# Down weights in 8 KB runs with strided transposes; inverse roots as one GpSimd power, small tables queued late, bias split moved to the router's end

## The chip, the cores and the metric

One core of a Trainium2 chip runs the whole layer. The metric is device time in microseconds (us), the median of the runs; every weight is read from HBM once, in float32. TensorE is called PE below (PEld is its weight load), VectorE DVE, ScalarE ACT, GpSimd POOL, and SP the engine whose queue issues nearly all DMAs.

## What is computed

A decoder layer on 256 tokens of width 1024: root-mean-square norm, one projection to seven groups of 512 columns, eight attention heads and four heads of a gated linear recurrence, an output projection, then a mixture of 32 experts (top 4 per token) and a per-layer embedding gate. Cut to what matters here:

```
def rms_norm(x, g):
    y = xf * lax.rsqrt(jnp.mean(xf * xf, axis=-1, keepdims=True) + RMS_EPS)
...
    a = rms_norm(h, mix_norm_g[i]);  z = a @ w_in[i]
    q = partial_rope(rms_norm(q, q_norm_g[i]), positions) * (ATTN_HEAD_DIM ** -0.5)
    k = partial_rope(rms_norm(k, k_norm_g[i]), positions)
...
    o = rms_norm(o, norm_g) * jax.nn.silu(gate)
...
    for e in range(N_EXPERTS):
        gu = t @ w_gu[e] + b_gu[e]
        ...
        y = ((up + 1.0) * glu) @ w_down[e] + b_down[e]
        out = out + gates[:, e:e + 1] * y
```

## The kernel before

The program has a front (norms, projection `zchunk`, attention, recurrence, output projection `wo`, router) and then a loop over the 32 experts, with a short end that applies the embedding gate.

**Weights.** All weights go through one list, `seq`, in the order of their use, as pieces of 1 MB. `fill` issues the next pieces on SP's queue as long as a slot is free; a slot is a piece of SBUF of 8 KB per partition, 19 of them at first (shared with the front's own tensors, which come from the same pool) and two more from the router on. `need` hands a piece to its user, and `used` frees its slot and calls `fill`. A gate/up piece is 128 rows, one row of 2048 numbers per partition, so one run of 8 KB in HBM. A down piece is 256 rows of 1024 numbers, and partition p gets rows p and 128 + p: two runs of 4 KB. In the front each piece of `w_in` and `w_out` is split into a rounded high part (ACT, line 193) and a rest (line 194, on DVE or, for the pieces in `POOL_FIRST`, on POOL).

**The inverse root.** `rsqrt` computes 1/sqrt by a bit trick and three Newton steps: 11 instructions on DVE on tiles of 128x2 to 128x16 (lines 245 to 250). It is used five times: for the rows of x (`row_rstd`), for k and q (`qk_norm`), for the recurrence's output (`hgrn_out`, r8) and for the second norm, whose result (rstd2) the router reads. The k and q norms stand between a projection chunk and the release of its PSUM tile: `pz` has two buffers, and line 608 (N) is the last reader of the chunk.

**Experts.** For each expert, `onehot` and `gather_rows` collect up to 64 tokens on PE, `gather_columns` transposes them, `gate_up` multiplies (line 1009 the bias, line 1016 the weights), `hidden` transposes the product u in four blocks of 128 columns (line 1034), `down` multiplies with the down weights (line 1047), and `scatter` adds to the result (line 1058). The bias is kept as a rounded part and its rest, `bgu`; the rest is made at the router's end on POOL (line 910).

A scheduler orders the instructions of each engine when the program is built. The lists in the section on the change print that order.

Of the kernel before, what the change touches and what calls it, by code (L numbers as in the profile page):

```python
# [11 lines left out]
F32 = mybir.dt.float32  # L12
F32R = mybir.dt.float32r
BF = mybir.dt.bfloat16
I32 = mybir.dt.int32
U32 = mybir.dt.uint32
AF = mybir.ActivationFunctionType
OP = mybir.AluOpType
# [4 lines left out]
E = 32  # L23
# [87 lines left out]
def layer(ctx, tc, A, at):  # L111
# [11 lines left out]
    seq, src = [], {}  # L123
# [10 lines left out]
        for n in range(2):  # L134
            add(("wo", n), hf, w_out, 512 * n)
    w_gu = A["expert_w_gate_up"][0].rearrange("e (j p) n -> e j p n", p=128)
    w_dn = A["expert_w_down"][0].rearrange("e (j k p) n -> e j p k n", p=128, k=2)

    def expert(kind, e):
        w, n = (w_gu, 8) if kind == "GU" else (w_dn, 4)  # L140
# [19 lines left out]
    def fill():  # L160
        while st["raw"] < st["cap"] and st["next"] < len(seq) and S.left() > st["keep"]:
            k = seq[st["next"]]
            st["next"] += 1
            st["raw"] += 1
            if k[0][0] == "GU":
                shape = [128, 2048]
            elif k[0][0] == "D" or k[0] == "pj":
                shape = [128, 2, 1024]
            else:
                shape = [128, 4, 512]  # L170
            t, at_ = S.new(shape, F32, "raw", True)
            sp.dma_start(t, src[k])
            raw[k] = t, at_

    def cap(n, keep=0):
# [58 lines left out]
    sp.dma_start(rows[16:24], A["hgrn_lb_logits"].rearrange("l (j p) -> (l j) p", p=128))  # L234
    gcol = pers.tile([128, 24], F32, name="gcol")

    def lnexp():
        act.preload_act_table_set("natural_log_exp_and_others")

    def rsqrt(y, v, tag):  # L240

        n = v.shape[1]
        a = pers.tile([128, n], F32, name="rs_a" + tag)
        b = pers.tile([128, n], F32, name="rs_b" + tag)
        dve.tensor_scalar(a.bitcast(I32), v.bitcast(I32), 1, None, op0=OP.arith_shift_right)
        dve.tensor_scalar(b.bitcast(I32), a.bitcast(I32), -1.0, float(0x5F3759DF), op0=OP.mult, op1=OP.add)
        for k in range(3):
            dve.scalar_tensor_tensor(a, v, -0.5, b, op0=OP.mult, op1=OP.mult)
            dve.tensor_tensor(a, a, b, OP.mult)
            dve.scalar_tensor_tensor(y if k == 2 else b, a, 1.5, b, op0=OP.add, op1=OP.mult)  # L250

    def row_rstd(tag):
        ss = pers.tile([128, 2], F32, name="ss" + tag)
        junk = S.new([128, 2, D], F32, "junk")
        for tt in range(2):
            act.activation(junk[:, tt, :], h[:, tt, :], AF.Square, accum_out=ss[:, tt:tt + 1])
        S.free()
        vv = pers.tile([128, 2], F32, name="vv" + tag)
        dve.tensor_scalar(vv, ss, 1.0 / D, EPS, op0=OP.mult, op1=OP.add)
        r = pers.tile([128, 2], F32, name="rstd" + tag)  # L260
        rsqrt(r, vv, tag)
        return r

    mx = ExitStack()
# [38 lines left out]
    sp.dma_start(pos_i, A["positions"].rearrange("o (t p) -> p (o t)", p=128))  # L303

    rw = mp.tile([128, 8, E], F32, name="rw")
    pool.dma_start(rw, A["router_w"][0].rearrange("(j p) e -> p j e", p=128))
    rb = mp.tile([128, E], F32, name="rb")
    pool.dma_start(rb, A["router_b"][0:1, :].to_broadcast([128, E]))
    tri = const("tri", q=pool, p=mp)
    slot = const("slot", q=pool)  # L310
    sel2 = const("sel", q=pool)

    p0 = bank()
    pe.transpose(p0[:, :24], rows, ident[:24, :24])
# [231 lines left out]
    def hgrn_out():  # L546
        vh = B["vh"]
        bs = [bank(), bank()]
        for hh in range(4):
            c = slice(hh * 128, hh * 128 + 128)  # L550
            c1 = slice(512 + hh * 128, 512 + hh * 128 + 128)
            pe.matmul(bs[0][:, c], B["A"][:, 0, hh, :], vh[:, c], start=True, stop=True)
            pe.matmul(bs[1][:, c], B["A01"][:, hh, :], vh[:, c], start=True, stop=False)
            pe.matmul(bs[1][:, c], B["A"][:, 1, hh, :], vh[:, c1], start=False, stop=True)
        S.free()
        values_read()
        B["ob"] = bs
        yield
        sq = carve(128)
        s8 = mp.tile([128, 8], F32, name="os8")  # L560
        for tt in range(2):
            for hh in range(4):
                act.activation(sq, bs[tt][:, hh * 128:hh * 128 + 128], AF.Square, accum_out=s8[:, tt * 4 + hh:tt * 4 + hh + 1])
        v8 = mp.tile([128, 8], F32, name="ov8")
        r8 = mp.tile([128, 8], F32, name="or8")
        dve.tensor_scalar(v8, s8, 1.0 / 128, EPS, op0=OP.mult, op1=OP.add)
        rsqrt(r8, v8, "o")
        B["r8"] = r8
        yield

# [24 lines left out]
    def qk_norm(p, gi, dst, scale):  # L595
        N2 = S.new([128, 2, 1024], F32, "N2")
        sq, n = N2[:, 0], N2[:, 1]
        act.activation(sq, p, AF.Square)
        yield
        s16 = mp.tile([128, 16], F32, name="s16")  # L600
        dve.tensor_reduce(s16, sq.rearrange("p (a d) -> p a d", d=64), X, OP.add)
        v16 = mp.tile([128, 16], F32, name="v16")
        dve.tensor_scalar(v16, s16, 1.0 / 64, EPS, op0=OP.mult, op1=OP.add)
        r16 = mp.tile([128, 16], F32, name="r16")
        rsqrt(r16, v16, "q%d" % gi)
        yield
        n3 = n.rearrange("p (a d) -> p a d", d=64)
        dve.tensor_tensor(n3, p.rearrange("p (a d) -> p a d", d=64), r16[:, :, None].to_broadcast([128, 16, 64]), OP.mult)  # L608
        dve.tensor_tensor(n3, n3, qg[:, gi:gi + 1, :].to_broadcast([128, 16, 64]), OP.mult)
        yield  # L610
        if "rt" not in B:
            B["rt"] = carve(384).rearrange("p (a b c d) -> p a b c d", a=2, b=3, c=8)
        r = B["rt"]
        for tt in range(2):
            v = n[:, tt * 512:tt * 512 + 512].rearrange("p (h d) -> p h d", d=64)
            x1, x2 = v[:, :, 0:8], v[:, :, 8:16]
            c = cs[:, tt, 0:1, :].to_broadcast([128, 8, 8])
            s = cs[:, tt, 1:2, :].to_broadcast([128, 8, 8])
            a, b_, c_ = (r[:, tt, k] for k in range(3))
            dve.tensor_tensor(a, x1, s, OP.mult)  # L620
            dve.tensor_tensor(b_, x1, c, OP.mult)
            dve.tensor_tensor(c_, x2, s, OP.mult)
            dve.tensor_tensor(x1, b_, c_, OP.subtract)
            dve.tensor_tensor(b_, x2, c, OP.mult)
            dve.tensor_tensor(x2, b_, a, OP.add)
        yield
        for h2 in range(2):
            b = bank()
            for k in range(2):
                for tt in range(2):  # L630
                    o = tt * 512 + (2 * h2 + k) * 128
                    pe.transpose(b[:, k * 256 + tt * 128:k * 256 + tt * 128 + 128], n[:, o:o + 128], ident)
            act.activation(dst[:, 2 * h2 * 256:2 * h2 * 256 + 512], b, AF.Copy, scale=scale)
        S.free()
        yield
# [181 lines left out]
    logits(1)  # L817
    dve.tensor_tensor(vv2, ss4[:, 0, :], ss4[:, 1, :], OP.add)
    dve.tensor_scalar(vv2, vv2, 1.0 / D, EPS, op0=OP.mult, op1=OP.add)
    rsqrt(rstd2, vv2, "m")  # L820

    S.free(3)
    cap(99)
# [83 lines left out]

    act.activation(bgu, braw, AF.Copy)
    for r in (slice(64, 96), slice(96, 128)):
        pool.tensor_tensor(bgu[r, :], braw[r, :], bgu[r, :].bitcast(F32), OP.subtract)  # L910
    spill()
    S.free(3)
    mx.close()
# [91 lines left out]
    def gate_up(e, between):  # L1005
        G, U = mm(), mm()
        x = R[e]["x"]
        for k, P in enumerate((G, U)):
            pe.matmul(P, R[e]["sel"], bgu[:, k * 512:k * 512 + 512], start=True, stop=False,  # L1009
                      skip_group_check=True)  # L1010
        for j in range(8):
            w, _ = need(("GU", e), j)
            for k, P in enumerate((G, U)):
                for n in range(2):
                    c = k * D + n * 512
                    pe.matmul(P[halves[n], :], x[:, j % 4, j // 4, :], w[:, c:c + 512], start=False, stop=j == 7, skip_group_check=True)  # L1016
            used(("GU", e), j, 0)
            for f in between.get(j, ()):
                f()
        gm = wp.tile([128, 512], F32, name="gm")  # L1020
        sg = wp.tile([128, 512], F32, name="sgm")
        um = wp.tile([128, 512], F32, name="um")
        dve.tensor_scalar(gm, G, 7.0, None, op0=OP.min)  # L1023
        act.activation(sg, gm, AF.Sigmoid, scale=1.702)  # L1024
        dve.tensor_scalar(um, U, 7.0, -7.0, op0=OP.min, op1=OP.max)
        dve.scalar_tensor_tensor(um, um, 1.0, gm, op0=OP.add, op1=OP.mult)
        dve.tensor_tensor(um, um, sg, OP.mult)
        R[e]["u"] = um

    def hidden(e):  # L1030
        u = R[e]["u"]
        b = misc()
        for c in range(4):
            pe.transpose(b[:, c * 128:c * 128 + 128], u[:, c * 128:c * 128 + 128], ident)  # L1034
        t = wp.tile([128, 4, 2, 64], F32, name="ht", bufs=2)
        act.activation(t.rearrange("p c n s -> p (c n s)"), b, AF.Copy)
        R[e]["h"] = t
# [155 lines left out]
```

## Time and profile before

| what | value |
|---|---|
| median of three runs | 1169.43 us (1166.47 to 1170.24) |
| the profiled execution's own time | 1167.22 us |
| its span, first to last instruction | 1165.4 us |
| PE busy | 93% of the span |
| DVE, ACT, POOL busy | 25%, 17%, 6% |
| HBM read | 430.51 MB, 370 GB/s over the span |
| TensorE clock granted, mean | 0.987 of full speed |

The profile is one execution. Busy shares are means over stages with different limits: the front lasts until about 190 us, the experts from there to about 1117 us. The end of a matmul is modelled, so a PE that is busy all the time may still have room.

### The profile page before, as it was taken

The numbers are of one execution on the slowest core, as the hardware profiler recorded it, in microseconds if no ns is written. First come the engines' busy times: TensorE is split into PE (matmuls) and PEld (weight loads), VectorE is DVE, ScalarE is ACT, GpSimd is POOL, SyncE is SP. The second block draws the span as 40 slices with busy tenths as digits, with TensorE's granted clock in tenths as the row PEclk, the third lists the DMA queues.
The fourth block names the chain that finished last, engine by engine and source line by source line (L and its number), as shares of the span: only waits on it lengthen the run. The fifth ranks groups of instructions, "written<-read, shape, count | busy, mean of one in ns | idle before, by whom it ended". The sixth has DMA issues, their size and how long they took to land. (4 is left out here: it accounts for less than half of the span.)

```text
span 1165.4 us, 12337 instructions
## 1 busy us (share of the span) xinstructions
PE 1080.2 (93%) x5001; PEld 451.9 (39%) x5001; DVE 294.1 (25%) x613; ACT 201.9 (17%) x366; POOL 74.8 (6%) x77
## 2 busy tenths in 40 slices
PE   5889988999999999999999999989999999999887
PEld 4778764333333333333333332223333332223226
DVE  4877744211111111111111111101111111110025
ACT  5646531000011011000000000001000000000013
POOL 4433321000000000000000000000000000000000
PEclk9989997999999999999999999999999999999999
DMA  9913568999999999999999999999998999999991
GB/s 313 338 60 103 207 227 324 415 416 417 417 416 417 417 418 418 417 417 418 417 417 417 417 417 417 405 417 417 416 415 327 418 417 417 417 418 417 418 400 46
DMA packets 87118, 432.43 MB, mean 371 GB/s; under 512 B 7736, under 2 KB 9184, under 8 KB 54288
## 3 DMA queue, kind: packets, MB, share of 16 engines
q1 hardware_dynamic: 86480, 430.35, 91.6%
q0 software_dynamic: 576, 1.23, 0.4%
q8 instruction: 41, 0.67, 0.2%
q14 instruction: 21, 0.17, 0.0%
HBM read 430.51 MB, written 1.05 MB: 370 GB/s over the span
## 5 line engine op out<-in xcount | busy, mean ns | idle before, releaser
L1016 PE MATMUL bk<-raw,x 128*64 128x512 f32 x2048 | 473.5, 596 | 12.5 <-DMA raw<-in_expert_w_gate_up 12.3
L1016 PEld LDWEIGHTS bk<-raw,x 128*64 128x64 f32 x2048 | 143.0, 137 | 311.6 <-issue 261.9
L1047 PE MATMUL bk<-raw,ht 128*64 128x512 f32 x1024 | 247.2, 598 | 12.5 <-DMA raw<-in_expert_w_down 12.5
L1047 PEld LDWEIGHTS bk<-raw,ht 128*64 128x64 f32 x1024 | 71.4, 136 | 150.9 <-issue 115.0
L1023 DVE TENSOR_SCALAR gm<-bk 128x512 f32<-128x512 f32 x32 | 22.1, 692 | 364.7 <-PE bk L1016 364.7
L1024 ACT ACTIVATE sgm<-gm 128x512 f32<-128x512 f32 x32 | 20.2, 630 | 422.5 <-DVE gm L1023 422.5
L846 PE MATMUL bk<-h,sx 128*64 128x512 f32 x256 | 66.1, 614 | 9.5 <-ACT st L1002 9.5
L997 DVE TENSOR_SCALAR sg<-c_slot,posx,gates 128x128 f32<-128x128 f32 x64 | 19.3, 344 | 213.1 <-PE bk L1000 213.1
L1058 PE MATMUL pz<-y,st 64*128 64x512 f32 x256 | 66.0, 627 | 4.0 <-ACT y L1051 2.2
L838 POOL CAST sb<-c_sel 128x128 fp32r<-128x128 f32 x32 | 9.3, 293 | 847.9 <-PE bk L1009 832.0
L194 POOL TENSOR_TENSOR lo<-raw,hi 128x1024 fp32r<-128x1024 f32 x20 | 50.1, 2526 | 84.7 <-ACT hi L193 84.7
L859 DVE TENSOR_TENSOR x<-bk,gcol 128x256 f32<-128x256 f32 x64 | 24.2, 420 | 108.8 <-PE bk L855 108.8
L1051 ACT ACTIVATE y<-bk 128x512 f32<-128x512 f32 x32 | 19.1, 597 | 145.5 <-PE bk L1047 145.5
L193 ACT ACTIVATE hi<-raw 128x1024 fp32r<-128x1024 f32 x36 | 37.8, 1056 | 22.9 <-issue 9.7
L1058 PEld LDWEIGHTS pz<-y,st 64*128 64x128 f32 x256 | 22.6, 188 | 45.7 <-issue 40.9
L380 PE MATMUL pz<-hi,ahi 128*128 128x512 f32 x80 | 33.6, 420 | 7.0 <-DVE N L608 6.8
L835 DVE TENSOR_SCALAR sx<-c_slot,posx,rstd 128x64 f32<-128x64 f32 x64 | 17.2, 312 | 79.0 <-PE bk L846 78.9
L848 ACT ACTIVATE xr<-bk 128x512 f32<-128x512 f32 x32 | 19.1, 597 | 93.7 <-PE bk L846 93.7
L382 PE MATMUL pz<-hi,alo 128*128 128x512 f32 x80 | 33.2, 415 | 0.0
L381 PE MATMUL pz<-lo,ahi 128*128 128x512 f32 x80 | 33.0, 412 | 0.0
L846 PEld LDWEIGHTS bk<-h,sx 128*64 128x64 f32 x256 | 17.4, 139 | 38.6 <-issue 24.4
L1002 ACT ACTIVATE st<-bk 128x256 f32<-128x256 f32 x32 | 12.3, 384 | 113.5 <-PE bk L1000 113.5
(266 smaller groups left out, 849.6 us busy)
## 6 DMA issues: line engine op xcount, KB each, us to landing
raw<-in_expert_w_gate_up SPq DMA_DIRECT2D x256, 1024.0 KB, 19.9
raw<-in_expert_w_down SPq DMA_DIRECT2D x128, 1024.0 KB, 20.0
raw<-in_w_in SPq DMA_DIRECT2D x14, 1024.0 KB, 13.6
raw<-in_w_out SPq DMA_DIRECT2D x4, 1024.0 KB, 5.1
raw<-in_ple_gate SPq DMA_DIRECT2D x4, 1024.0 KB, 18.9
h<-in_x SPq DMA_DIRECT2D x2, 512.0 KB, 4.2
ct<-in_consts SPq DMA_DIRECT2D x2, 512.0 KB
raw<-in_ple_proj SPq DMA_DIRECT2D x1, 1024.0 KB, 20.2
```

The lines of the kernel that those rows point to most:

```text
L193: act.activation(hi, w[:, o:o + 2], AF.Copy)
L194: (pool if i in POOL_FIRST else dve).tensor_tensor(lo, w[:, o:o + 2], hi.bitcast(F32), OP.subtract)
L380: pe.matmul(o, ahi[:, j, s], hi[:, jj, :], start=j == 0, stop=False)
L381: pe.matmul(o, ahi[:, j, s], lo[:, jj, :], start=False, stop=False)
L382: pe.matmul(o, alo[:, j, s], hi[:, jj, :], start=False, stop=j == 7)
L846: pe.matmul(b[halves[n], :], s[:, tt, :], h[:, tt, n * 512:n * 512 + 512], start=tt == 0, stop=tt == 1, skip_group_check=True)
L859: dve.tensor_tensor(x[:, :, n, :], b.rearrange("p (c n s) -> p c n s", c=4, n=2)[:, :, n, :], g, OP.mult)
L1016: pe.matmul(P[halves[n], :], x[:, j % 4, j // 4, :], w[:, c:c + 512], start=False, stop=j == 7, skip_group_check=True)
L1023: dve.tensor_scalar(gm, G, 7.0, None, op0=OP.min)
L1024: act.activation(sg, gm, AF.Sigmoid, scale=1.702)
L1047: pe.matmul(P[halves[n], :], t[:, f % 4, f // 4, :], w[:, k, n * 512:n * 512 + 512], start=f == 0, stop=f == 7, skip_group_check=True)
L1058: pe.matmul(acc[tt][n], t[halves[n], tt * 128:tt * 128 + 128], y[halves[n], :], start=e == 0, stop=False, skip_group_check=True)
```

## The change

It does six things. (1) The down weights are read with partition p holding rows 2p and 2p + 1 of the piece, one run of 8 KB; `hidden` therefore transposes every second column of u. (2) `rsqrt` becomes one instruction on POOL, v to the power -0.5. (3) In `row_rstd` the second half of the squares goes from ACT to DVE. (4) The first piece of `w_in` is loaded by two DMAs of half the size. (5) The five small tables (router weights, router bias, tri, slot, sel) go from POOL's DMA queue to SP's, behind the first six pieces. (6) The rest of the bias is made on DVE instead of POOL, and the bias of expert 0 is multiplied after its weights instead of before.

```
-    w_dn = A["expert_w_down"][0].rearrange("e (j k p) n -> e j p k n", p=128, k=2)
+    w_dn = A["expert_w_down"][0].rearrange("e (j p k) n -> e j p k n", p=128, k=2)
...
-            sp.dma_start(t, src[k])
+            if place[k]:
+                sp.dma_start(t, src[k])
+            else:
+                for o in (0, 2):
+                    sp.dma_start(t[:, o:o + 2], src[k][:, o:o + 2])
...
+    power = pers.tile([128, 16], F32, name="power")
+    pool.memset(power, -0.5)
...
-    def rsqrt(y, v, tag):
-
-        n = v.shape[1]
-        a = pers.tile([128, n], F32, name="rs_a" + tag)
-        b = pers.tile([128, n], F32, name="rs_b" + tag)
-        dve.tensor_scalar(a.bitcast(I32), v.bitcast(I32), 1, None, op0=OP.arith_shift_right)
-        dve.tensor_scalar(b.bitcast(I32), a.bitcast(I32), -1.0, float(0x5F3759DF), op0=OP.mult, op1=OP.add)
-        for k in range(3):
-            dve.scalar_tensor_tensor(a, v, -0.5, b, op0=OP.mult, op1=OP.mult)
-            dve.tensor_tensor(a, a, b, OP.mult)
-            dve.scalar_tensor_tensor(y if k == 2 else b, a, 1.5, b, op0=OP.add, op1=OP.mult)
+    def rsqrt(y, v):
+        pool.tensor_tensor(y, v, power[:, :v.shape[1]], OP.pow)
...
-        for tt in range(2):
-            act.activation(junk[:, tt, :], h[:, tt, :], AF.Square, accum_out=ss[:, tt:tt + 1])
+        act.activation(junk[:, 0, :], h[:, 0, :], AF.Square, accum_out=ss[:, 0:1])
+        dve.scalar_tensor_tensor(junk[:, 1, :], h[:, 1, :], 1.0, h[:, 1, :], op0=OP.mult, op1=OP.mult, accum_out=ss[:, 1:2])
...
-    pool.dma_start(rw, A["router_w"][0].rearrange("(j p) e -> p j e", p=128))
+    sp.dma_start(rw, A["router_w"][0].rearrange("(j p) e -> p j e", p=128))
...
-        pool.tensor_tensor(bgu[r, :], braw[r, :], bgu[r, :].bitcast(F32), OP.subtract)
+        dve.tensor_tensor(bgu[r, :], braw[r, :], bgu[r, :].bitcast(F32), OP.subtract)
...
+        def bias():
+            for k, P in enumerate((G, U)):
+                pe.matmul(P, R[e]["sel"], bgu[:, k * 512:k * 512 + 512], start=e > 0, stop=e == 0, skip_group_check=True)
...
-            pe.transpose(b[:, c * 128:c * 128 + 128], u[:, c * 128:c * 128 + 128], ident)
+            o = c // 2 * 256 + c % 2
+            pe.transpose(b[:, c * 128:c * 128 + 128], u[:, o:o + 255:2], ident)
```

On POOL, from the start of the program to the end of the router, the order before was this (`lo` is a split of line 194, `rw` the router's weights, `braw` the raw bias, `sb` an expert's selector).

```order
L306 DMA rw<-in_router_w 128x8x32
L308 DMA rb<-in_router_b 128x32
L225 DMA c_tri<-in_consts 128x128
L741 TENSOR_TENSOR rw<-rw,gcol 128x256
L194 TENSOR_TENSOR lo<-raw,hi 128x1024 x9
L463 MEMSET Adg 128x1024
L194 TENSOR_TENSOR lo<-raw,hi 128x1024 x9
L780 DMA braw<-in_expert_b_gate_up 32x512 x8
L194 TENSOR_TENSOR lo<-raw,hi 128x1024 x2
L838 CAST sb<-c_sel 128x128 x2
L910 TENSOR_TENSOR bgu<-braw,bgu 32x1024 x2
```

The same stretch of POOL's order now has the five powers (line 248: for x, k, q, the recurrence's output and the router).

```order
L248 TENSOR_TENSOR rstdx<-vvx,power 128x2
L198 TENSOR_TENSOR lo<-raw,hi 128x1024 x6
L739 TENSOR_TENSOR rw<-rw,gcol 128x256
L248 TENSOR_TENSOR r_341<-v_339,power 128x16
L198 TENSOR_TENSOR lo<-raw,hi 128x1024 x3
L461 MEMSET Adg 128x1024
L198 TENSOR_TENSOR lo<-raw,hi 128x1024
L248 TENSOR_TENSOR r_576<-v_574,power 128x16
L198 TENSOR_TENSOR lo<-raw,hi 128x1024 x8
L778 DMA braw<-in_expert_b_gate_up 32x512 x8
L248 TENSOR_TENSOR or_1190<-ov_1189,power 128x8
L198 TENSOR_TENSOR lo<-raw,hi 128x1024 x2
```

The tables' DMAs are gone from POOL, each power stands between splits, and the bias's rest is no longer there.

On DVE, at the start of the program, the order now is this (`ssx` are the sums of squares, `vvx` the mean square, `lbm` and `lbe` belong to the recurrence's lower bound and read `gcol`, `mt` is the diagonal that PE's first transposes read).

```order
L254 SCALAR_TENSOR_TENSOR junk,ssx<-h 128x1024
L419 TENSOR_TENSOR lbm<-gcol 128x4
L257 TENSOR_SCALAR vvx<-ssx 128x2
L421 TENSOR_TENSOR lbe<-gcol,lbm 128x4
L422 TENSOR_TENSOR lbe<-gcol,lbm 128x4
L318 TENSOR_SCALAR mt<-c_ident,rstdx 128x128 x2
```

The mean square, which was DVE's first instruction, now stands behind one that waits for `gcol`.

On DVE, at the router's end, the order before was this (`hT` is h transposed, `vv` the mean square, `rs_am` and `rs_bm` the Newton steps).

```order
L801 COPY hT<-bk 128x512
L818 TENSOR_TENSOR vv_1445<-ss_1354 128x2
L819 TENSOR_SCALAR vv_1445<-vv_1445 128x2
L245 TENSOR_SCALAR rs_am<-vv_1445 128x2
L246 TENSOR_SCALAR rs_bm<-rs_am 128x2
L801 COPY hT<-bk 128x512
L248 SCALAR_TENSOR_TENSOR rs_am<-vv_1445,rs_bm 128x2
```

The same place now:

```order
L799 COPY hT<-bk 128x512
L908 TENSOR_TENSOR bgu<-braw,bgu 32x1024 x2
L816 TENSOR_TENSOR vv_1400<-ss_1309 128x2
L799 COPY hT<-bk 128x512
L817 TENSOR_SCALAR vv_1400<-vv_1400 128x2
```

The two bias instructions now stand ahead of the second copy of `hT`, and the Newton steps are gone.

## Rows read from the trace of the kernel before

**Rows 1.** The page: span, GB/s in 40 slices of the span.
```profile
span 1165.4 us, 12337 instructions
...
GB/s 313 338 60 103 207 227 324 415 416 417 417 416 417 417 418 418 417 417 418 417 417 417 417 417 417 405 417 417 416 415 327 418 417 417 417 418 417 418 400 46
```

**Rows 2.** Window 365-700: start:end, length, PE, PEld, DVE, ACT, POOL, clock, DMA share, GB/s.
```profile
365.00:700.00 335.00, 321.25 (x1480) 108.45 (x1476) 55.98 (x120) 33.66 (x60) 3.52 (x12) 1.00 1.02 417
```

**Rows 3.** Waits of PE over the whole span: total us, times, longest.
```profile
PE bk L1047 <- DMA raw<-in_expert_w_down: 12.5, 19, 1.6
PE bk L1016 <- DMA raw<-in_expert_w_gate_up: 12.3, 24, 0.6
```

**Rows 4.** PE's timeline (start, us): the same place of two experts that follow each other.
```profile
398.68 0.63 PE L1034 MATMUL bk<-c_ident,um 128*128 128x128 f32 x4 [0.69 <-DVE um L1027]
...
426.81 0.63 PE L1034 MATMUL bk<-c_ident,um 128*128 128x128 f32 x4 [0.69 <-DVE um L1027]
```

**Rows 5.** Windows, first with only 4 KB runs in flight, then with only 8 KB runs.
```profile
250.00:258.00 8.00, 8.00 (x40) 2.73 (x38) 1.29 (x4) 0.60 (x1) 0.00 (x0) 1.00 1.03 410
...
260.20:278.00 17.80, 17.80 (x84) 6.13 (x82) 1.55 (x4) 1.57 (x3) 0.29 (x1) 1.00 1.01 421
```

**Rows 6.** DMA issues of the down weights; the weight loads of line 1034.
```profile
raw<-in_expert_w_down SPq DMA_DIRECT2D x128, 1024.0 KB, 20.0
...
L1034 PEld LDWEIGHTS bk<-c_ident,um 128*128 128x128 f32 x128 | 13.4, 141 | 36.7 <-issue 18.7 <-PE bk L1047 18.0
```

**Rows 7.** Timeline of the start, DVE and POOL.
```profile
7.08 0.17 DVE L259 TENSOR_SCALAR vvx<-ssx 128x2 f32<-128x2 f32 x1 [7.08 <-ACT junk L256]
...
8.59 0.16 DVE L421 TENSOR_TENSOR lbm<-gcol 128x4 f32<-128x4 f32 x1 [0.93 <-ACT gcol L315]
8.64 0.61 POOL L741 TENSOR_TENSOR rw<-rw,gcol 128x256 f32<-128x256 f32 x1 [3.94 <-ACT gcol L315]
...
10.96 0.48 DVE L320 TENSOR_SCALAR mt<-c_ident,rstdx 128x128 f32<-128x128 f32 x2
```

**Rows 8.** PE's waits in the front (0 to 210 us), columns as in rows 3.
```profile
PE pz L380 <- DVE N L608: 6.8, 2, 3.6
PE bk L806 <- DVE hT L801: 3.1, 2, 2.0
PE bk L584 <- DVE G L578: 2.1, 2, 1.9
```

**Rows 9.** Windows in the front, columns as in rows 2.
```profile
72.80:79.70 6.90, 6.79 (x19) 5.41 (x20) 6.87 (x18) 0.56 (x2) 0.00 (x0) 0.62 0.15 55
...
159.60:164.40 4.80, 4.80 (x14) 3.80 (x15) 1.22 (x2) 0.42 (x1) 0.00 (x0) 0.64 0.80 297
```

**Rows 10.** Timeline of DVE in the k norm.
```profile
37.32 2.46 DVE L603 TENSOR_SCALAR v<-s 128x16 f32<-128x16 f32 x1
...
41.48 2.37 DVE L248 SCALAR_TENSOR_TENSOR rs_aq<-v,rs_bq 128x16 f32<-128x16 f32 x1
...
44.38 1.23 DVE L608 TENSOR_TENSOR N<-pz,r 128x1024 f32<-128x1024 f32 x1
```

**Rows 11.** Timeline of DVE: q norm, the recurrence's output.
```profile
64.57 2.40 DVE L603 TENSOR_SCALAR v<-s 128x16 f32<-128x16 f32 x1
...
71.54 1.23 DVE L608 TENSOR_TENSOR N<-pz,r 128x1024 f32<-128x1024 f32 x1
...
150.08 0.17 DVE L566 TENSOR_SCALAR ov<-os 128x8 f32<-128x8 f32 x1 [1.51 <-ACT mt L563]
...
156.84 2.16 DVE L578 SCALAR_TENSOR_TENSOR G<-bk,or,G 128x128 f32<-128x128 f32 x8
```

**Rows 12.** Timeline of the router's end, DVE and POOL.
```profile
173.85 4.78 POOL L910 TENSOR_TENSOR bgu<-braw,bgu 32x1024 fp32r<-32x1024 f32 x2 [0.61 <-POOL sb L838]
...
176.47 2.19 DVE L245 TENSOR_SCALAR rs_am<-vv 128x2 int32<-128x2 int32 x1
178.77 0.68 DVE L801 COPY hT<-bk 128x512 f32<-128x512 f32 x1
```

More of the change, by code (lines that the diff above doesn't have):

```diff
@@ L260, in row_rstd @@
         r = pers.tile([128, 2], F32, name="rstd" + tag)
-        rsqrt(r, vv, tag)
+        rsqrt(r, vv)
         return r
@@ L305, in layer @@
     rw = mp.tile([128, 8, E], F32, name="rw")
-    pool.dma_start(rw, A["router_w"][0].rearrange("(j p) e -> p j e", p=128))
+    sp.dma_start(rw, A["router_w"][0].rearrange("(j p) e -> p j e", p=128))
     rb = mp.tile([128, E], F32, name="rb")
[L308 to L311, printed above, removed]
+    sp.dma_start(rb, A["router_b"][0:1, :].to_broadcast([128, E]))
+    tri = const("tri", p=mp)
+    slot = const("slot")
+    sel2 = const("sel")
     p0 = bank()
@@ L566, in hgrn_out @@
         dve.tensor_scalar(v8, s8, 1.0 / 128, EPS, op0=OP.mult, op1=OP.add)
-        rsqrt(r8, v8, "o")
+        rsqrt(r8, v8)
         B["r8"] = r8
@@ L604, in qk_norm @@
         r16 = mp.tile([128, 16], F32, name="r16")
-        rsqrt(r16, v16, "q%d" % gi)
+        rsqrt(r16, v16)
         yield
@@ L819, in layer @@
     dve.tensor_scalar(vv2, vv2, 1.0 / D, EPS, op0=OP.mult, op1=OP.add)
-    rsqrt(rstd2, vv2, "m")
+    rsqrt(rstd2, vv2)
     S.free(3)
@@ L1007, in gate_up @@
         x = R[e]["x"]
-        for k, P in enumerate((G, U)):
-            pe.matmul(P, R[e]["sel"], bgu[:, k * 512:k * 512 + 512], start=True, stop=False,
-                      skip_group_check=True)
+        def bias():
+            for k, P in enumerate((G, U)):
+                pe.matmul(P, R[e]["sel"], bgu[:, k * 512:k * 512 + 512], start=e > 0, stop=e == 0, skip_group_check=True)
+        if e:
+            bias()
         for j in range(8):
@@ L1015, in gate_up @@
                     c = k * D + n * 512
-                    pe.matmul(P[halves[n], :], x[:, j % 4, j // 4, :], w[:, c:c + 512], start=False, stop=j == 7, skip_group_check=True)
+                    pe.matmul(P[halves[n], :], x[:, j % 4, j // 4, :], w[:, c:c + 512], start=e == 0 and j == 0, stop=j == 7 and e > 0,
+                              skip_group_check=True)
             used(("GU", e), j, 0)
@@ L1019, in gate_up @@
                 f()
+        if not e:
+            bias()
         gm = wp.tile([128, 512], F32, name="gm")
```

## The prediction

> **What bounds the kernel now.** I read the page's slices first. Its 40 columns of GB/s fall in two parts: the first seven, some 190 us, go from 313 down to 60 and up again, and from the eighth to the thirty-eighth nearly all read 415 to 418 [rows 1]. A rate that is the same in slice after slice while the work of the experts differs is a transfer that runs without a break. The window of the middle says so directly: DMA share 1.02, PE 321 of 335 us, clock 1.00 [rows 2]. PE looks nearly as full, so I asked the view of the waits who waits for whom. PE waits for expert weights 12.5 + 12.3 = 24.8 us in 43 pieces [rows 3]; the other way round there is little, since the rate does not sag. PE's own pace is seen between two places of the timeline where it had not waited for a DMA: 426.81 − 398.68 = 28.13 us per expert [rows 4]. DMA's pace is 12 pieces of 1.0486 MB, 12.58 MB, at 417 GB/s [rows 2]: 30.2 us. So the experts go at the speed of the transfer, with PE 2 us per expert behind in need. In the front it is the other way: the rate is low there because all slots are full and PE frees them slowly. Hence two things alone move the end: the rate of the expert weights, and the moment at which the front begins to release slots at full pace. A microsecond taken from the front's PE path comes off the end in full, as long as the experts stay bound by DMA.
>
> **Down weights as 8 KB runs.** The trace has both forms side by side. Where only down pieces (4 KB runs) were in flight I read 410 GB/s, in five windows of five; where only gate/up pieces (8 KB runs) were, 420 to 422, five again, 421 in the mean; one of each is shown [rows 5]. The mixture fits: 8 pieces at 421 and 4 at 410 take 19.9 + 10.2 = 30.1 us, which is the 417 of the long window [rows 2]. The down weights are 128 pieces [rows 6], 134.2 MB: 327.4 us at 410 and 318.8 at 421. That is −8.6; the first few down pieces come while the rate is still low, so **−8.5**. The bounds are nothing (the rate stays 410, if it is not the run length that sets it) and −8.6. The Trainium skill says in "DMA: Bandwidth & Descriptors", section "Why small descriptors are slow (HBM only)", that each packet carries a fixed overhead of about 3 cycles beside one cycle per 32 bytes; estimated from that page, 131 against 2 × 131 − 3 = 259 cycles for 8 KB is 1.1%, −3.7 us, and the sum below would be 1155. The rows show 2.7%, so the rows decide.
>
> **Strided transposes.** Four per expert. The transposed block is PE's weight load, 141 ns for 128 columns [rows 6], now every second column. Nothing in the trace strides a load. Lower bound nothing; upper bound, each load doubled: 4 × 0.141 = 0.56 us per expert. The cover is PE's reserve, the 24.8 us that it waits for expert weights [rows 3]; the faster transfer takes 8.5 of it, 16.3 are left, 0.127 us for each of 128 loads. Doubled loads cost 18.0 and would show with 1.7. I count nothing, since 141 ns for 128 columns is already about the time of any load here.
>
> **The power instead of Newton's steps.** No power stands in the trace. The nearest row is a POOL tensor-tensor of 128 x 256 with 0.61 us [rows 7]; for 2 to 16 columns I take 0.6. Bounds: 0.1, and 2.4, half of POOL's 4.78 for two instructions of 1024 columns [rows 12]. What it replaces:
>
> - Start. The mean square was ready at 7.08 + 0.17 and the diagonal `mt` began at 10.96 [rows 7]. In the new order the mean square stands behind `lbm`, which waits for `gcol` and starts at 8.59. So 8.59 + 0.16 + 0.17, then 0.6 and a hand-over of some 0.1: 9.65. **−1.3**. The second sum of squares on DVE hides behind that same wait.
> - k norm. From the end of `v` (37.32 + 2.46 = 39.78) to N at 44.38 are 4.6 us; one of the small steps took 2.37 instead of the 0.17 of others, beside a POOL split [rows 10]. PE waits for N in two places, 6.8 us, at most 3.6 [rows 8]. By the power's 0.7 the chain becomes 3.9 shorter, more than the wait: the shorter wait, **−3.2**, goes.
> - q norm. 64.57 + 2.40 to 71.54: 4.6 us [rows 11]; PE's wait is the longer, 3.6, so **−3.5**. After it the clock stands at 0.62 for 6.9 us [rows 9], a loss of 6.9 × 0.38 = 2.6. PE was idle before the fall; with the idle time gone I count the loss as gone too: **−2.6**.
> - Recurrence. From `ov` (150.25) to G at 156.84 are 6.6 us [rows 11]; PE waits for G 2.1 [rows 8] and then runs at 0.64 for 4.8 us [rows 9], a loss of 1.7. With the small holes beside it **−2.3** and **−1.7**.
>
> **Router's end.** POOL's two bias instructions run from 173.85 for 4.78, and a DVE step of two columns that starts in this time takes 2.19 and ends with them (178.66); the second `hT` copy starts at 178.77 [rows 12]. PE waits 3.1 for `hT` [rows 8]. On DVE the two cost 1.23 each (the row of N, also 1024 columns [rows 10]); 174.5 + 2.46 = 177.0, so `hT` comes **−1.7** earlier. The bias of expert 0 now ends its chain instead of beginning it: four matmuls, the same number; I count nothing, bounds ±0.8.
>
> **Tables and the split first piece.** Five small issues go ahead of piece 7 on SP and delay what stands behind them by 5 × 0.3 to 0.6 us; the front is not bound by DMA (60 to 227 GB/s in slices 3 to 6 [rows 1]), so they are hidden. Without that cover they cost up to 3 us. Half a piece that lands earlier lets the split start earlier, but PE's first product still waits for the diagonal: nothing.
>
> **Sum.** The front: 1.3 + 3.2 + 3.5 + 2.6 + 2.3 + 1.7 + 1.7 = 16.3. Against it stands what the powers meet on POOL, which takes its instructions in order: three of them come behind splits of some 2.4 us, which a power that becomes ready late enough must wait out. No wait leaves −16.3, a whole split each (7.2) −9.1; I take three quarters, −5.4, hence **−11**. 1167.2 (the profiled execution's own time; its span is 1165.4 [rows 1]) − 8.5 − 11 = 1147.7. The median of the runs before lies 2.2 above this execution: **1150**.
>
> **Rivals.** A measurement of this kernel can tell about 0.3% from no change, 3.5 us: faster is below 1165.9, slower above 1172.9.
>
> A, both parts as above: 1150, own range 1143 (no waits on POOL) to 1157 (each power 2.4 and a split's wait).
>
> B, the front's gain is taken by another wait. For it: DVE runs the recurrence's chains and the splits beside the norms, and the clock may fall somewhere else. Against: PE's waits for N and G are named in the trace. Then the rate alone is left: 1167.2 − 8.5 + 2.2 = 1161 (1158 to 1164).
>
> C, the first power waits for its code. POOL stood idle 3.94 us before its first tensor-tensor [rows 7], put down to `gcol`, so a load could have been hidden there. The first power is at the start, where all wait for it: up to +3.9, 1154. The Trainium skill says in "GPSIMD Engine Reference", § 2.1 Instruction dispatch, that the first call to a freshly loaded kernel pays approximately 6 us; by it the time would be 1156, and no row before shows it.
>
> D, strided loads make PE the bound: it decides from +0.127 us per load on. At three times 141 ns, 128 × 0.282 = 36 us less the reserve of 16.3: 1150 + 20 = 1170. For it: the reserve is small; against: nothing in the trace tells that a load depends on the step of its columns.
>
> E, on the other side: the power is slow. It replaces 3.9 + 4.6 + 4.6 + 6.6 = 19.7 us of chains. Four of p each make the front longer by 4p − 19.7; with the −8.5 of the rate the kernel gets slower from p = 7.0. At p = 8.5 it is 1169.4 − 8.5 + 14.3 = 1175. For it: an unknown function on POOL; against: POOL does 1024 columns in 2.4 us, and here are 2 to 16.
>
> **How the numbers follow.** A 0.58, B 0.20, C 0.08, D 0.04, E 0.10. Predicted is A, 1150. The range 1141 to 1163 holds A, C and nearly all of B, 0.84; outside lie D, E and the ends. Faster: A, B, C and the smaller half of D, 0.87; the rest of D and E with a power near 7 make the same, 0.07; E beyond it slower, 0.06.
>
> **What the profile after would show.** If right: windows of down pieces at 421 like the others, packets under 8 KB fewer by 128 × 256 = 32768, an expert's period near 29.9; powers below 1 us; the wait L380 for N nearly gone and no stretch at 0.62 behind it; the front's last GB/s dip ending some 10 us earlier; L1034's loads near 141 ns. The prediction is wrong if the down windows stay at 410 (the run length is not what sets the rate), if a power shows several us, if PE waits as long as before for another releaser, or if PE's waits for expert weights fall from 24.8 to nothing instead of some 16 (PE is the bound).

## The result and the profile after

The changed kernel took 1148.75 us in the median of 5 runs (1147.74 to 1150.07), the kernel before 1166.58 beside it (1165.86 to 1170.24): ratio 0.9844, interval 0.9827 to 0.9861. 1150 had been predicted. The profiled execution spans 1146.0 us instead of 1165.4, 19.4 less. Clock means are 0.988 and 0.987.

The page of the kernel after, span and GB/s in 40 slices:

```profile
span 1146.0 us, 12292 instructions
...
GB/s 312 361 86 147 190 306 372 366 420 420 419 419 420 420 420 420 420 420 420 420 420 419 419 420 420 409 420 419 420 414 356 420 420 420 420 419 420 420 401 42
```

Beside [rows 1] the plateau stands at 420 instead of 417. The way up runs ahead (306 and 372 where 227 and 324 stood), but the eighth slice has a dent of 366 that was not there, so the plateau itself begins one slice later, with the ninth. Two more views answer to [rows 2, 3]. The window of the middle (start:end, length, PE, PEld, DVE, ACT, POOL, clock, DMA share, GB/s):

```profile
365.00:700.00 335.00, 321.48 (x1478) 109.52 (x1474) 55.40 (x118) 33.30 (x59) 3.53 (x12) 1.00 1.01 420
```

and PE's waits over the span (total us, times, longest):

```profile
PE bk L1017 <- DMA raw<-in_expert_w_gate_up: 10.1, 18, 0.7
...
PE bk L1052 <- DMA raw<-in_expert_w_down: 7.6, 14, 0.7
...
PE pz L378 <- DVE N L606: 3.4, 1, 3.4
```

The transfer is still the bound; PE's waits for expert weights fell from 24.8 to 17.7 us, where some 16 had been forecast.

Where the 19.4 us lie is read best from a ladder of places that both timelines have. All are starts, in us of each kernel's own profiled execution ("gate/up, expert 1" is that expert's first gate/up product, "last gate/up" the latest of all):

| kernel | mt | N of k | N of q | ov | G | gather, expert 0 | u transposed, expert 0 | gate/up, expert 1 | last gate/up |
|---|---|---|---|---|---|---|---|---|---|
| before | 10.96 | 44.38 | 71.54 | 150.08 | 156.84 | 187.52 | 212.65 | 213.68 | 1108.3 |
| after | 8.08 | 34.88 | 62.04 | 141.32 | 143.27 | 171.25 | 199.41 | 201.18 | 1089.3 |
| difference | −2.9 | −9.5 | −9.5 | −8.8 | −13.6 | −16.3 | −13.2 | −12.5 | −19.0 |

The front ends 16.3 us earlier, expert 0 gives 3.8 of them back, and from expert 1 on the faster transfer takes off 6.5. The powers on GpSimd, in the timeline of the kernel after:

```profile
7.33 0.71 POOL L248 TENSOR_TENSOR rstdx<-vvx,power 128x2 f32<-128x2 f32 x1 [6.34 <-DVE lbe L422]
...
31.94 2.90 POOL L248 TENSOR_TENSOR r<-v,power 128x16 f32<-128x16 f32 x1 [0.18 <-DVE v L601]
...
59.11 2.90 POOL L248 TENSOR_TENSOR r<-v,power 128x16 f32<-128x16 f32 x1 [2.52 <-DVE v L601]
...
141.58 1.66 POOL L248 TENSOR_TENSOR or<-ov,power 128x8 f32<-128x8 f32 x1 [4.09 <-DMA raw<-in_expert_w_gate_up]
...
164.39 0.69 POOL L248 TENSOR_TENSOR rstd<-vv,power 128x2 f32<-128x2 f32 x1 [4.72 <-DVE vv L817]
```

A power costs 0.7 us for 2 columns, 1.66 for 8 and 2.90 for 16: by these rows 0.16 us for each column on top of 0.4. None of the five is kept waiting by a split; before three of them GpSimd stood idle for several us. (The fifth stands behind the end of the list of POOL's order in the section on the change.)

DVE's timeline of the kernel after, the recurrence's output, to hold against [rows 11]:

```profile
141.32 0.17 DVE L564 TENSOR_SCALAR ov<-os 128x8 f32<-128x8 f32 x1 [2.55 <-ACT mt L561]
143.27 2.16 DVE L576 SCALAR_TENSOR_TENSOR G<-bk,or,G 128x128 f32<-128x128 f32 x8 [1.78 <-POOL or L248]
```

From `ov` to G are 1.95 us instead of 6.76. The k norm, to hold against [rows 10]:

```profile
31.70 0.16 DVE L601 TENSOR_SCALAR v<-s 128x16 f32<-128x16 f32 x1
...
34.88 1.22 DVE L606 TENSOR_TENSOR N<-pz,r 128x1024 f32<-128x1024 f32 x1 [0.18 <-POOL r L248]
```

And PE's timeline in the q norm, which stayed as bad as before:

```profile
63.41 0.77 PE L378 MATMUL pz<-hi,ahi 128*128 128x512 f32 x1 [3.36 <-DVE N L606]
...
65.69 0.63 PE L380 MATMUL pz<-hi,alo 128*128 128x512 f32 x1
...
66.79 0.39 PE L380 MATMUL pz<-hi,alo 128*128 128x512 f32 x1
```

PE still waits 3.36 us for N and then runs at a low granted clock (a mean of 0.53 from 63.4 to 66.8 us, 1.00 from 66.8 on; a product takes 0.63 instead of 0.39), but only for some 3 us, not the 6.9 of [rows 9].

### The profile page after: what moved, and what is told of

Its sections match the earlier page's. It is cut to its first block, busy times and chain, and to the rows that moved or that the text cites. A ratio compares the mean times of both kernels' runs of the same rounds, so it can differ in the third digit from the quotient of the medians.

```text
span 1146.0 us, 12292 instructions
## 1 busy us (share of the span) xinstructions
PE 1075.5 (94%) x5001; PEld 451.7 (39%) x5001; DVE 285.9 (25%) x562; ACT 200.2 (17%) x364; POOL 81.8 (7%) x76
## 5 line engine op out<-in xcount | busy, mean ns | idle before, releaser
L198 POOL TENSOR_TENSOR lo<-raw,hi 128x1024 fp32r<-128x1024 f32 x20 | 56.0, 2819 | 46.9 <-ACT hi L197 37.4
L1039 PE MATMUL bk<-c_ident,um 128*128 128x128 f32 x128 | 23.7, 309 | 11.2 <-DVE um L1031 11.1
L844 PEld LDWEIGHTS bk<-h,sx 128*64 128x64 f32 x256 | 17.7, 139 | 39.0 <-issue 26.8
## 6 DMA issues: line engine op xcount, KB each, us to landing
ct<-in_consts SPq DMA_DIRECT2D x2, 512.0 KB, 11.3
```

The lines of the kernel that those rows point to most:

```text
L198: (pool if i in POOL_FIRST else dve).tensor_tensor(lo, w[:, o:o + 2], hi.bitcast(F32), OP.subtract)
L844: pe.matmul(b[halves[n], :], s[:, tt, :], h[:, tt, n * 512:n * 512 + 512], start=tt == 0, stop=tt == 1, skip_group_check=True)
L1039: pe.transpose(b[:, c * 128:c * 128 + 128], u[:, o:o + 255:2], ident)
```

## The experiments

Times are medians; ratios are to the kernel before, run beside them on the same chip (1167.6 to 1168.6 in these three groups of runs). The ladder of the runs that the text uses; each row is one execution. The first run has the code of the kernel before in its front and still stands up to 2.8 us later on the way to G, so a difference of two or three us between two rows says little by itself.

| kernel | mt | N of k | N of q | ov | G | gather, expert 0 | u transposed, expert 0 | last gate/up |
|---|---|---|---|---|---|---|---|---|
| down only (first) | 11.3 | 46.0 | 74.4 | 151.90 | 158.66 | 188.9 | 216.5 | 1103.3 |
| bias first (third) | 8.2 | 34.5 | 62.0 | 143.10 | 145.1 | 172.5 | 197.6 | 1087.3 |
| Newton (fourth) | 13.20 | 46.87 | 75.79 | 153.52 | 160.2 | 189.2 | 217.5 | 1107.6 |
| power alone (fifth) | 8.3 | 40.4 | 64.6 | 141.81 | 143.76 | 169.72 | 194.7 | 1085.5 |
| tables on POOL (sixth) | 11.3 | 41.8 | 66.0 | 142.45 | 144.4 | 172.3 | 200.5 | 1091.1 |
| k and q alone (eleventh) | 10.2 | 40.14 | 67.42 | 148.77 | 155.47 | 186.1 | 211.3 | 1101.6 |

**The two halves of the change.** First, the kernel before with the down weights alone:

```
-    w_dn = A["expert_w_down"][0].rearrange("e (j k p) n -> e j p k n", p=128, k=2)
+    w_dn = A["expert_w_down"][0].rearrange("e (j p k) n -> e j p k n", p=128, k=2)
...
-            pe.transpose(b[:, c * 128:c * 128 + 128], u[:, c * 128:c * 128 + 128], ident)
+            o = c // 2 * 256 + c % 2
+            pe.transpose(b[:, c * 128:c * 128 + 128], u[:, o:o + 255:2], ident)
```

> The kernel before with the 8 KB runs of the down weights and the strided transposes alone. Theory (run length sets the rate, and the rate is the bound): the period of an expert falls from 30.13 us to about 29.92, 32 times 0.21 is 6.7, the front is unchanged: about 7 us below the kernel before, ratio 0.994. Rival (the gain of the rate came only together with the shorter front, or the strided loads, now 209 ns instead of 141, eat it): no change, ratio 1.000.

Measured: 1158.74, ratio 0.9919 (0.9901 to 0.9937). The front's ladder is not earlier, and the middle moves at 421 GB/s:

```profile
365.00:700.00 335.00, 321.04 (x1474) 109.24 (x1472) 55.92 (x120) 33.68 (x60) 3.55 (x12) 1.00 1.01 421
```

Second, the changed kernel with just these lines taken back:

> The changed kernel with the down weights in 4 KB runs and plain transposes again. Theory (front and rate add): about 12 us below the kernel before, ratio 0.990, with the first product of expert 0 some 16 us earlier and that of expert 1 some 12 us earlier. Rival (the front's gain is hidden behind the transfer): within 4 us of the kernel before, ratio 0.997 or more.

Measured: 1156.87, ratio 0.9901 (0.9881 to 0.9921); the middle stands at 416:

```profile
365.00:700.00 335.00, 318.78 (x1460) 106.66 (x1462) 54.89 (x119) 33.05 (x59) 3.23 (x11) 1.00 1.02 416
```

Both theories hold and both rivals fall: 0.9919 × 0.9901 is 0.9821, against 0.9844 for the whole. The halves add, to within the intervals.

**What the run length costs.** The eighth run reads the same down weights in 2 KB runs (kernel before; the products of down are then of permuted weights):

```
-    w_dn = A["expert_w_down"][0].rearrange("e (j k p) n -> e j p k n", p=128, k=2)
+    w_dn = A["expert_w_down"][0].rearrange("e (j k p) (h n) -> e j p h k n", p=128, k=2, h=2)
```

> The kernel before with the down weights in runs of 2 KB (the same bytes, in another order within a piece, so the products of down are of permuted weights). Theory (each packet costs a fixed time beside its bytes: 163.6 ns for 4 KB and 315.4 for 8 KB in the traces of before and after are 11.8 fixed and 37.95 per KB, so 87.7 ns for 2 KB, 351 instead of 327 per 8 KB): the down pieces at some 378 GB/s, 20 to 28 us slower than the kernel before, ratio 1.017 to 1.024. Rival (the rate steps up only between 4 and 8 KB): no change, ratio 1.000.

Measured: 1188.55, ratio 1.0173 (1.0147 to 1.0199). Windows of that run, the first with only 2 KB runs in flight, the second with only 8 KB runs (columns as above):

```profile
252.00:258.00 6.00, 6.00 (x30) 2.12 (x28) 0.76 (x2) 0.00 (x0) 0.00 (x0) 1.00 1.05 387
...
263.00:281.00 18.00, 18.00 (x84) 6.24 (x82) 1.14 (x4) 2.16 (x4) 0.29 (x1) 1.00 1.01 418
```

With 410 and 421 of [rows 5] that is 387, 410, 421 for 2, 4 and 8 KB. Per piece of 1.0486 MB these are 2.71, 2.56 and 2.49 us: halving the run from 8 to 4 KB adds 0.07, from 4 to 2 KB 0.15, twice as much for twice as many runs. A fixed cost per run does just that. The Trainium skill's overhead of some 3 cycles per packet ("DMA: Bandwidth & Descriptors", section "Why small descriptors are slow (HBM only)") would make 2 KB cost about 7.5 us over 4 KB, an estimate from the page; 20.7 were measured, so for this transfer the fixed part is larger than the page says.

**The price of the strided loads.** In the kernel after (line of the tile's users: duration min/median/max in ns, first and last start):

```profile
L1039 PEld LDWEIGHTS bk<-c_ident,um x128: 194/209/230, 199.4 to 1092.7; 128*128 128x128 f32 x128
```

209 ns instead of 141 [rows 6]: every second column costs a load 68 ns, 8.7 us of weight loading in all. The tenth run goes back to neighbouring columns with the 8 KB runs kept (the products of down are then of permuted values):

```
-            o = c // 2 * 256 + c % 2
-            pe.transpose(b[:, c * 128:c * 128 + 128], u[:, o:o + 255:2], ident)
+            pe.transpose(b[:, c * 128:c * 128 + 128], u[:, c * 128:c * 128 + 128], ident)
```

> The changed kernel with the transposes of u reading neighbouring columns again, so that the products of down are of permuted values. It measures the price of the strided weight loads, 209 ns in the changed kernel. Theory (128 loads of 68 ns more, 8.7 us of PE's time, lie under the transfer, since PE waits for expert weights 17.7 us): within 1.5 us of the changed kernel, loads back at 141 ns, PE's waits for expert weights up by 5 to 9 us. Rival (they stand on the path): 4 to 9 us faster than the changed kernel.

Measured: 1150.19, ratio 0.9853 (0.9838 to 0.9867): no gain. The weight loads of that run:

```profile
L1038 PEld LDWEIGHTS bk<-c_ident,um x128: 137/141/143, 199.3 to 1092.4; 128*128 128x128 f32 x128
```

and its waits of PE over the span:

```profile
PE bk L1017 <- DMA raw<-in_expert_w_gate_up: 11.0, 20, 0.7
...
PE bk L1051 <- DMA raw<-in_expert_w_down: 9.7, 16, 1.2
```

The waits grow from 17.7 to 20.7 only, 3 where 5 to 9 were expected: the forecast of no gain held, its size for the waits did not. That part of the 68 ns was already under other work of PE is argued, not shown.

**What the power is worth.** The fourth run is the changed kernel with Newton's eleven DVE steps back in `rsqrt`, all else as changed.

> The changed kernel with the eleven DVE instructions of the inverse root in place of the GpSimd power, all else as changed. Theory (the power shortens the k and q chains by 1.6 us each, the recurrence's output by some 4, the start by about 1): 4 to 8 us slower than the changed kernel, 1153 to 1157. Rival (the front's gain came from the start, where rows and the first piece land earlier, and the powers bring little, since those of 16 columns take 2.9 us): within 2 us of the changed kernel.

Measured: 1165.23, ratio 0.9973 (0.9963 to 0.9984): over the changed kernel 15 us by the ratios, 16.5 by the medians. Neither side had it: not 4 to 8, and not 2. It is even 6.5 us slower than the first run, which has the front of before. DVE's timeline at the start of that run:

```profile
9.10 0.16 DVE L258 SCALAR_TENSOR_TENSOR rs_a<-vvx,rs_b 128x2 f32<-128x2 f32 x1
9.93 1.23 DVE L198 TENSOR_TENSOR lo<-raw,hi 128x1024 fp32r<-128x1024 f32 x1 [0.66 <-ACT hi L197]
...
11.14 0.15 DVE L259 TENSOR_TENSOR rs_a<-rs_a,rs_b 128x2 f32<-128x2 f32 x1
...
11.41 1.23 DVE L198 TENSOR_TENSOR lo<-raw,hi 128x1024 fp32r<-128x1024 f32 x1
...
13.01 0.16 DVE L260 SCALAR_TENSOR_TENSOR rstdx<-rs_a,rs_b 128x2 f32<-128x2 f32 x1
13.20 0.48 DVE L330 TENSOR_SCALAR mt<-c_ident,rstdx 128x128 f32<-128x128 f32 x2
```

Eleven steps that depend on each other are eleven places in DVE's order where something else can stand between, and here two splits of the earlier first piece do, one of them waiting for ACT. `mt` comes at 13.20 instead of 8.08. The split that arrives early delays the root. That is not what makes the 6.5 us, though: at expert 0's gather the two runs stand within 0.3 us (189.2 and 188.9). Behind it the fourth run has the bias of expert 0 last, and from 200 to 230 us its transfer moves 351 GB/s against 382 in the first (see the edits of the bias below).

The fifth run turns it round: the first run (8 KB runs) plus the power, without the five other edits of the front.

```
-        dve.tensor_scalar(a.bitcast(I32), v.bitcast(I32), 1, None, op0=OP.arith_shift_right)
...
+        pool.tensor_tensor(y, v, power[:, :v.shape[1]], OP.pow)
```

> The kernel before with the 8 KB runs and strided transposes of the first experiment (1158.7) and the GpSimd power, without the five other edits of the front. Theory (the power takes the eleven steps out of DVE's queue, and that is nearly all of the front's gain): 1149 to 1152. Rival (half of it comes from the start: the tables off GpSimd's queue and the halved first piece): 1154 to 1157, the first diagonal mt still near 10 us.

Measured: 1145.62, ratio 0.9806 (0.9780 to 0.9832). Both forecasts were too high. The power alone takes 13.1 us off the first run's 1158.74, and the five other edits together bring nothing beside it: this kernel is at least as fast as the changed one, and its median is the lowest of all that were run.

**Which of the five powers.** The eleventh run is the first run's kernel with the power for k and q alone.

```
+        if tag[0] == "q":
+            pool.tensor_tensor(y, v, power[:, :v.shape[1]], OP.pow)
+            return
```

> The first experiment's kernel (1158.7) with the power for the norms of k and q alone; x, the recurrence's output and the router keep Newton's steps. With all five powers it was 1145.6. Theory of the prediction's terms (k 3.2, q 3.5 and 2.6 of clock, against 1.3 for x and 4.0 for the recurrence): k and q are some 60 per cent of the 13.1, 1150 to 1152. Rival (a 16-column power takes 2.9 us, so that k and q gain little, and what counts is the recurrence's output and the router behind it): 1154 to 1157.

Measured: 1159.16, ratio 0.9925 (0.9911 to 0.9939), against 0.9919 (0.9901 to 0.9937) without any power. Neither forecast had it. The norms of k and q, 9.3 us of the predicted sum, bring by themselves nothing that stands out of the intervals. The ladder shows the loss: N of q is 6.9 us earlier than in the first run, `ov` only 3.1. PE's waits of that run in the front show what came instead:

```profile
PE pz L385 <- DVE N L613: 3.0, 1, 3.0
...
PE bk L589 <- DVE G L583: 2.3, 2, 2.1
PE bk L533 <- DVE W L507: 1.9, 1, 1.9
...
PE bk L533 <- DVE Adg L537: 1.0, 1, 1.0
```

The two waits of line 533 for the recurrence's tiles W and Adg are new (before, PE waited for neither): PE reaches the recurrence earlier than DVE has it ready. (The changed kernel has both, with 1.8 and 1.5 us.) The output's chain stayed long, 6.7 us from `ov` to G:

```profile
148.77 0.17 DVE L571 TENSOR_SCALAR ov<-os 128x8 f32<-128x8 f32 x1 [2.69 <-ACT mt L568]
...
150.60 2.32 DVE L253 SCALAR_TENSOR_TENSOR rs_ao<-ov,rs_bo 128x8 f32<-128x8 f32 x1
152.95 2.29 DVE L254 TENSOR_TENSOR rs_ao<-rs_ao,rs_bo 128x8 f32<-128x8 f32 x1
...
155.47 2.16 DVE L583 SCALAR_TENSOR_TENSOR G<-bk,or,G 128x128 f32<-128x128 f32 x8
```

Two steps of 8 columns took 2.3 instead of 0.17 us, both beside GpSimd's splits (4.73 us from 150.49). With all five powers G stands 11.7 us earlier and expert 0's gather 16.4: 4.8 of it is the chain from `ov` to G, 4.7 the way from G to the gather (30.7 against 26.0 us), the rest lies ahead of `ov`. That the gain belongs to the other three powers is so far a subtraction; they were not run without those of k and q.

**The start.** Sixth, the tables on GpSimd's queue again; seventh, the first piece in one DMA:

```
-    sp.dma_start(rw, A["router_w"][0].rearrange("(j p) e -> p j e", p=128))
+    pool.dma_start(rw, A["router_w"][0].rearrange("(j p) e -> p j e", p=128))
...
-    tri = const("tri", p=mp)
+    tri = const("tri", q=pool, p=mp)
```

> The changed kernel with the five small tables on GpSimd's queue again. Theory (they slow the first transfers: the rows of the norms land 1.8 us later, as before): 2 to 4 us slower than the changed kernel, about 1151 to 1153, first transpose of the rows at 8 instead of 6.3 us. Rival (PE's start is not what the front's end hangs on): within 1 us of the changed kernel.

Measured: 1149.66, ratio 0.9836 (0.9814 to 0.9859).

```
-            if place[k]:
-                sp.dma_start(t, src[k])
-            else:
-                for o in (0, 2):
-                    sp.dma_start(t[:, o:o + 2], src[k][:, o:o + 2])
+            sp.dma_start(t, src[k])
```

> The changed kernel with the first piece of w_in loaded by one DMA. Theory (the first split starts some 2 to 3 us later, but PE has its 32 transposes of h until about 14 us): within 1 us of the changed kernel. Rival (the first products wait for the split): 1 to 3 us slower.

Measured: 1150.00, ratio 0.9843 (0.9821 to 0.9866). Neither edit shows in the time. The tables do delay the start: `mt` is at 11.3. N of k is at 41.8, 6.9 us after the changed kernel's, but that is mostly something else: the norm's `v` starts only 0.5 us later (32.18 against 31.70). GpSimd's timeline behind it:

```profile
34.31 2.90 POOL L248 TENSOR_TENSOR r<-v,power 128x16 f32<-128x16 f32 x1
37.18 4.68 POOL L198 TENSOR_TENSOR lo<-raw,hi 128x1024 fp32r<-128x1024 f32 x2
```

Beside these two splits two small steps that stand ahead of N in DVE's order take 2.39 and 2.26 us (0.18 and 0.17 in the changed kernel); the fifth run has the same (2.01 and 2.28). At G 1.1 us are left of the 6.9. What the front gains ahead of the q norm is waited away before the recurrence's output, as in the eleventh run.

**The two edits of the bias.** Third, the bias of expert 0 ahead of its weights; ninth, its rest on GpSimd; twelfth, both.

```
-        if e:
-            bias()
+        bias()
...
-        if not e:
-            bias()
```

> The changed kernel with the bias of expert 0 ahead of its weights again, as in the other experts. Theory (the bias at the end lengthens expert 0: 0.7 us of matmuls, a wait of 2.8 for um and a stretch at a clock of 0.69 behind it): 2 to 4 us faster than the changed kernel, about 1146. Rival (the wait for um stands there with either order, as it did before with 2.4): within 1 us of the changed kernel, 1148 to 1150.

Measured: 1146.00, ratio 0.9826 (0.9799 to 0.9853).

```
-        dve.tensor_tensor(bgu[r, :], braw[r, :], bgu[r, :].bitcast(F32), OP.subtract)
+        pool.tensor_tensor(bgu[r, :], braw[r, :], bgu[r, :].bitcast(F32), OP.subtract)
```

> The changed kernel with the rest of the bias made on GpSimd again. Theory of the prediction (the DVE form brings the second hT copy 1.7 us earlier): 1 to 2 us slower than the changed kernel, 1150 to 1151. Rival (without Newton's steps nothing on DVE is left there to be stretched; on DVE the two instructions of 1.2 us hold up the second hT copy, PE idles and the clock falls to 0.56 behind it): 1 to 3 us faster, 1146 to 1148, clock at 165 to 170 us above 0.9.

Measured: 1146.57, ratio 0.9828 (0.9812 to 0.9845).

> The changed kernel with two edits taken back: the bias of expert 0 ahead of its weights and the rest of the bias on GpSimd. Theory (both edits cost, about 2.5 and 1 to 3 us): 1143 to 1145. Rival (both act through the same low clock at the router's end, so that one of them taken back gives all): about 1146, the same as with the bias alone taken back.

Measured: 1147.02, ratio 0.9821 (0.9805 to 0.9837). All three medians lie 1.7 to 2.8 us under the changed kernel's, and all three intervals overlap with its own, so in time it is only likely that each edit costs, and not shown that both together cost more than one. (For both together the rival's 1146 is the nearer forecast. In the ninth run the rival's time came, but not its clock: 0.78 from 165 to 170 us, not above 0.9.) The traces say more. For the first edit, PE's timeline of the changed kernel in expert 0:

```profile
195.91 0.73 PE L1008 MATMUL bk<-bgu,sb 128*128 128x512 f32 x2
199.41 0.98 PE L1039 MATMUL bk<-c_ident,um 128*128 128x128 f32 x4 [2.77 <-DVE um L1031]
```

From gather to the transposes of u it takes 28.2 us, 25.1 in the kernel before and 25.1 with the bias first. About 1.0 of the 3.0 are the two bias matmuls and a wait for `um` of 2.77 instead of 2.40. The other 2.0 lie ahead of expert 1's gather: the first weight products start 0.5 us later and run at a mean granted clock of 0.88, where the kernel before and the third run have 1.00. The first run, with the bias first, falls to 0.84 there too and takes 27.6, so the low clock does not come with the late bias alone. What this costs at the end is seen in the transfer. The slices of the third run:

```profile
GB/s 315 367 80 144 171 315 382 412 419 419 419 420 419 420 420 420 419 420 419 420 419 419 419 420 419 411 420 419 419 406 348 421 420 419 420 420 420 419 403 42
```

The dent in the eighth slice is gone: 412 instead of 366. All seven kept traces with the bias last (the changed kernel and the second, fourth, sixth, seventh, ninth and tenth runs) read 356 to 366 there, all seven with the bias first 392 to 420. From 200 to 230 us the changed kernel moves 368 GB/s and the third run 412, which at 420 is 3.1 us of transfer, about what the medians differ by.

For the second edit, the way from G to the gather: with all five powers it takes 27.4 to 29.1 us in the six traces with the rest on DVE and 26.0 to 27.0 in the three with the rest on GpSimd (fifth, ninth, twelfth). The window behind the router (165 to 170 us, columns as above) of the changed kernel reads:

```profile
165.00:170.00 5.00, 3.25 (x18) 3.01 (x17) 2.33 (x20) 0.53 (x2) 0.08 (x1) 0.56 0.96 370
```

and of the fifth run, in which the rest is on GpSimd as before:

```profile
165.00:170.00 5.00, 2.78 (x21) 2.52 (x22) 3.50 (x25) 0.54 (x2) 1.13 (x2) 0.93 0.78 306
```

The clock is 0.56 against 0.93, after a hole of 0.5 us in PE's work while DVE does the bias ahead of the second `hT` copy. That the hole drops the clock is not shown. Taken at the same distance from the gather (6.25 to 1.25 us ahead of it), the clock is 0.56 in the changed kernel, 1.00 in the fifth run and 0.95 in the ninth, but 0.69 in the twelfth, with the rest on GpSimd, and 0.76 in the third, with the rest on DVE.

## Why the prediction was right, step by step

The time, the sign and the two halves came out: 8.5 for the transfer and 11 for the front were forecast; the halves alone measured 9.5 and 11.6 by their ratios (0.9919 and 0.9901 of 1168). The terms inside the front did not come out as they were written, and the front's sum is right because its errors cancel, which is luck. Of the signs named, the rate and the waits for expert weights came; the powers below 1 us (up to 2.90) and the loads of the transposes near 141 ns (209) did not, and the wait for N went by half.

- **The rate**: right. 420 GB/s against 421. The eighth run shows that it is the run length.
- **Strided transposes**: "I count nothing" held for the time, but not for its reason, that a load would stay near 141 ns. It grew by 0.068 us, half of the 0.127 that the reserve allowed.
- **The price of a power**, 0.6 with bounds of 0.1 and 2.4: right for 2 columns (0.7), too low for 8 (1.66), and for 16 (2.90) above the upper bound. The row I took it from was an elementwise product, which told nothing of a power's cost for each column.
- **Start, −1.3**: measured −2.9, as the rows of the norms landed earlier too (PE's first transpose at 6.28 instead of 8.06), and worth little at the end (sixth run).
- **k norm −3.2, q norm −3.5 and −2.6**: this is the step that failed. By the prediction's measure, from the end of `v` to N of k, the chain went from 4.6 to 3.0 us, 1.6 shorter and not 3.9, because the power took 2.90 and not 0.6. From the start of `v` it is 3.9 shorter (7.06 to 3.18), but the rest of that is `v` itself, 2.46 us before [rows 10] and 0.16 now, which the sum did not count. Of PE's two waits the one at k went. The one at q stayed with 3.36, since the gain at k was used up before q (the q norm's chain began 5.7 us earlier, where N of k was 9.5), and alone the two gain nothing at the end that can be told from noise (eleventh run).
- **Recurrence −2.3 and −1.7**: right and too small. The chain shrank by 4.8, the wait for G is no longer among PE's waits and the clock behind it stays at 1.00 up to 160 us.
- **Router's end −1.7**: gained, 2.7 from G's step to the gather, but not by the bias on DVE. Where Newton's steps stand, that edit gains about what was forecast, in the one trace that has both: 29.0 us from G to the gather in the fourth run against 30.2 to 30.7 in the kernel before and the first, eighth and eleventh runs. With the power it costs (27.4 to 29.1 against 26.0 to 27.0). My sum counted nothing for the fifth power, which takes the stretched Newton step of 2.19 us in [rows 12] out of `hT`'s way by itself.
- **5.4 back for powers behind splits**: did not occur; no power waited for a split. What the traces show against the gain in its place are the longer powers, the new waits for W and Adg (3.3 us together) and the bias of expert 0. By the sum's own terms A without these waits is 1144.6, not the 1143 that the range of A gives.
- **Bias of expert 0**, counted as nothing with ±0.8: costs 3.0 us of expert 0 by the trace. As first instruction it had run while PE waited for x; as last it stands between the weights and the chain that makes u, which is 1.0 of the 3.0. The other 2.0 are the low clock ahead of it, whose cause stays open.

Of the rivals, C (a first power that waits for code) fell: the first power took 0.71, the fifth, of the same size, 0.69; no run here shows the 6 us of the Trainium skill ("GPSIMD Engine Reference", § 2.1 Instruction dispatch). D and E did not come near. B, the front's gain taken by another wait, is false for the sum and true for its first half.

Left open: what k and q are worth once the other three powers are there (only their share alone was run), and the 4 us that the fifth run gains over the eleventh between N of q and `ov`.

## What to carry to other kernels

A chain of small dependent instructions costs more than its length: each step is a place where the engine's order can put something else, and where a step can be caught beside another engine's large one (0.17 us became 2.3). One slower instruction on an idle engine in place of each chain, even at 2.9 us, took 13 to 16 us off this kernel. Before summing the terms of a front, ask of each where its gain is waited away: here the gains of k and q did not reach the end by themselves, and the chains behind them (the recurrence's output and the router) are the likely place of the rest. And where a transfer is the bound, longer runs can be worth their price on another engine: here 8.7 us of longer weight loads, against 17.7 us in which PE waits for weights, cost no time.

## What was not expected of the hardware

GpSimd's power has a price for each column, some 0.16 us for 128 rows, beside 0.4 fixed: 0.7, 1.66 and 2.90 us for 2, 8 and 16 columns. A weight load of every second float32 column takes 209 ns instead of 141. And 2, 4 and 8 KB runs move at 387, 410 and 421 GB/s, the same bytes by the same queue.
